# An encoder layer on one core: the first up-projection weights, their sums and one pair's first products moved into the end of the stage before

## The chip, the cores and the metric

The kernel runs on one core of one Trainium2 chip. A core has a matrix engine (TensorE; PE in the profile, its weight loads PEld), VectorE (DVE), ScalarE (ACT), GpSimd (POOL), an engine that only issues transfers (SyncE, SP), and DMA engines that move data between HBM and the core's memory, SBUF. Matrix products are written to PSUM, in banks of 128 x 512 f32.

The metric is the time of one execution in microseconds, as the device measures it. Every kernel was run several times; the median is given with the lowest and the highest.

## What is computed

One layer of an encoder for two sequences of 512 tokens (1024 rows) of width 1024, all in f32. A first part makes `mixed` from a windowed attention branch and a state-space branch; the change lies behind it, in the last two lines:

```python
    x = x + mixed @ w_out                                   # 1024 x 1024
    h2 = rms_norm(x, ln2)
    return x + jnp.square(jax.nn.relu(h2 @ w_up)) @ w_down  # 1024 x 4096, 4096 x 1024
```

## The kernel before

**Products.** Each f32 operand is split into a part that is rounded for the matrix engine (`hi`, a copy on ScalarE) and the remainder (`lo`, a subtraction on VectorE). One product of blocks is then three matmuls, `hi hi`, `hi lo`, `lo hi` (`mm3`, lines 114 to 118, so L116, L117 and L118 of the profile). With four blocks of inner size 128 a product in the up projection is 12 matmuls of 128 x 512.

**The output projection with the norm (L1222 to L1332).** `out_half(x1, sq, t, b)` makes the 128 rows `t` of sequence `sq` for column half `b`: 24 matmuls, then an addition to the residual rows on VectorE (L1238). The halves of `w_out` lie as rounded parts in `w_rows[0]` (pool `wpool`, two tiles tagged `act0` and `act1`, 16 KB per partition each) and `w_rows[1]` (pool `slot_a`, likewise). When both halves of the rows are there they are stored to `x1_scr` (L1325, issued by ScalarE) and normalised by `norm_of`: a square with a row sum on ScalarE (L1255), two small operations on GpSimd that make the power -1/2 (L1257, L1258), and a scaling on VectorE (L1259).

**The turn.** `turn_of` transposes the normalised rows on TensorE (L1273), eight 128 x 128 blocks into two PSUM banks, and `put` writes the rounded part (ScalarE, L1266) and remainder (VectorE, L1267) of the right-hand operands of the up projection. For sequence 0 these are B11 and B21. For sequence 1, which has the other half of the tokens, they are B22 and the combinations T1, T2, T4, T3, made in this order (L1284 to L1293) in two scratch blocks `tt[0]` and `tt[1]`. Each is complete after the turn of the last rows (`t` = 3). The turn of a block of rows is written behind the first `out_half` of the next block, so that TensorE has products to do while the norm is made. For the last rows the cover is `first_products`, below.

**The up projection (L1343 to L1423).** `w_up` comes in 16 pairs of 256 columns, each as a 2 x 2 block `a11 a21 a12 a22` (`raw`, four blocks of 128 x 512, 1 MB in two loads of 512 KB, L1390). A pair needs seven products instead of eight (Strassen's scheme in Winograd's form): p1 = a11 B11, p2 = a21 B21 (the first two of `raw`), p6 = s2 T2, p7 = s3 T3, p5 = s1 T1, p3 = s4 B22, p4 = `raw[:, 3]` T4, with the sums s1 to s4 made by VectorE from the raw blocks (`sums`, L1378 to L1385). `parts` splits a block into a slot of an eight-slot ring (L1346 to L1351, so L1349 on ScalarE and L1350 on VectorE). The results are combined on VectorE (`combine`, L1364), pass a squared ReLU on ScalarE (L1370, L1371) and are stored to `a_scr`.

**Pairs 0 and 1 at the seam.** p1 and p2 of the first two pairs are made in the stage before, by `first_products` (L1296 to L1308): it makes p1, copies it out of PSUM on ScalarE (L1306), makes p2 and adds both on VectorE (L1304). They need only blocks a11 and a21, which are loaded separately (`up_parts`, L1245 to L1250, tile `f_raw`). Pair 0's parts are made early into tiles of their own (`ws`). Pair 1's parts go into `wpool`'s two tiles when `w_rows[0]` is no longer read (`early`, L1327 and L1328). At the end stand: `first_products(ws)`, the last turn, `first_products(ws_1)`. Then `wpool` is closed, and the pool `up` is opened over its memory and that of the stage's work tiles (`rn2`). The whole 1 MB of pair 0 and of pair 1 is then loaded into `up`'s `u_raw` buffers, two of them, and pair 0's sums and parts are made from it.

**What sets the order.** TensorE's order in this stage is the written one (`manual_schedule(engines={ET.PE})`, L1311, until `order.close()`, L1332). On the other engines, and on TensorE in the up projection, a scheduler at compile time takes the written order as priority and puts later work into gaps that it sees. Whatever order results, an engine then keeps it. A tile whose memory was another's waits until that one was last used.

Of the kernel before, what the change touches and what calls it, by code (L numbers as in the profile page):

```python
# [12 lines left out]
F32 = mybir.dt.float32  # L13
# [6 lines left out]
P = 128  # L20
# [4 lines left out]
KT = D // P  # L25
NSEQ = 2
HALF = 512
# [36 lines left out]
def hybrid_layer(ctx, tc, x, rel, onehot, w_qkv, w_ug, vectors, lam, coefs, w_glu, w_out, ln2,  # L64
                 w_up, w_down, out):
    nc = tc.nc
    V, S, PE, GP, SP = nc.vector, nc.scalar, nc.tensor, nc.gpsimd, nc.sync
# [58 lines left out]
    def slot(pool):  # L126
        return [pool.tile([P, KT, HALF], F32R, tag=f"act{i}", name=f"act{i}") for i in range(2)]
# [140 lines left out]
    order = ctx.enter_context(ExitStack())  # L268
# [954 lines left out]
    with tc.tile_pool(name="rn2", bufs=2, reuse_waits="tile") as rn2:  # L1223
        ln2_bc = rn2.tile([P, D], F32, name="ln2_bc", bufs=1)
        SP.dma_start(ln2_bc, ln2.to_broadcast([P, D]))
        for k in range(KT):
            row_piece(w_rows[1], 1, k, rn2.tile([P, HALF], F32, tag="w_raw", name="w_raw", bufs=3))

        def rows_of(sq, t):
            return slice((sq * 4 + t) * P, (sq * 4 + t + 1) * P)  # L1230

        def out_half(x1, sq, t, b):
            ps = acc()
            for k in range(KT):
                mm3(ps, [q[:, k, t * P:(t + 1) * P] for q in mixT[sq]], [q[:, k, :] for q in w_rows[b]],
                    k == 0, k == KT - 1)
            xs = x1[:, b * HALF:(b + 1) * HALF]
            V.tensor_add(xs, ps, xs)  # L1238

        def load_rows_of(sq, t):  # L1240
            x1 = rn2.tile([P, D], F32, tag="x1", name="x1")
            SP.dma_start(x1, x[rows_of(sq, t), :])
            return x1

        def up_parts(r, i, hi, lo):  # L1245
            raw = rn2.tile([P, 4, P], F32, tag="w_raw", name="f_raw", bufs=3)
            SP.dma_start(raw, w_up[r, :, i])
            S.copy(hi, raw)
            V.tensor_sub(lo, raw, hi.bitcast(F32))
            return hi, lo  # L1250

        def norm_of(x1):
            xn = rn2.tile([P, D], F32, tag="xn", name="rn_xn", bufs=1)
            ss = small.tile([P, 1], F32, tag="ss", name="ss")
            S.activation(xn, x1, AF.Square, scale=D ** -0.5, accum_out=ss)  # L1255
            rs = small.tile([P, 1], F32, tag="rs", name="rs")
            GP.tensor_scalar_add(ss, ss, EPS)  # L1257
            GP.tensor_tensor(rs, ss, neg_half[:, 0:1], op=ALU.pow)  # L1258
            V.scalar_tensor_tensor(xn, x1, rs, ln2_bc, op0=ALU.mult, op1=ALU.mult)  # L1259
            return xn  # L1260

        def turn_of(sq, t, xn):
            cs = slice(t * P, (t + 1) * P)

            def put(dst, src):
                S.copy(dst[0][:, :, cs], src)  # L1266
                V.tensor_sub(dst[1][:, :, cs], src, dst[0][:, :, cs].bitcast(F32))  # L1267

            for kq in range(2):
                ps = tps() if sq == 0 else sps()  # L1270
                for i in range(4):
                    kk = kq * 4 + i
                    PE.transpose(ps[:, i * P:(i + 1) * P], xn[:, kk * P:(kk + 1) * P], ident)  # L1273
                xb.append(ps.rearrange("p (k t) -> p k t", k=4))
            if sq == 0:
                put(B11, xb[0])
                put(B21, xb[1])
                return
            tx = rn2.tile([P, 2, 4, P], F32, tag="xn", name="tx", bufs=1)
            tt = [tx[:, 0], tx[:, 1]]  # L1280
            x11, x21, x12, x22 = xb
            put(B22, x22)

            S.copy(tt[0], x11)  # L1284
            V.tensor_sub(tt[0], x12, tt[0])
            put(T1, tt[0])
            V.tensor_sub(tt[1], x22, tt[0])
            put(T2, tt[1])
            V.tensor_sub(tt[1], tt[1], x21)
            put(T4, tt[1])  # L1290
            S.copy(tt[0], x22)
            V.tensor_sub(tt[0], tt[0], x12)
            put(T3, tt[0])  # L1293
            xb.clear()

        def first_products(ws):  # L1296
            sums = []
            for w, b in zip(ws, (B11, B21)):
                ps = acc()
                for k in range(4):  # L1300
                    mm3(ps, [q[:, k, :] for q in w], [q[:, k, :] for q in b], k == 0, k == 3)
                d = fpre.tile([P, HALF], F32, tag="f_lo" if sums else "f_hi", name="f_sum")
                if sums:
                    V.tensor_add(d, ps, sums[0])  # L1304
                else:
                    S.copy(d, ps)  # L1306
                sums.append(d)
            first.append(sums)  # L1308

        xb, owed = [], None  # L1310
        order.enter_context(tc.manual_schedule(engines={ET.PE}))  # L1311
        x1s = [load_rows_of(sq, 0) for sq in range(NSEQ)]
        for sq in range(NSEQ):
            out_half(x1s[sq], sq, 0, 0)
        ws = [up_parts(0, i, *[fpre.tile([P, 4, P], F32R, tag=tag, name=tag) for tag in ("f_hi", "f_lo")]) for i in range(2)]
        for t in range(NT // 2):
            if t:
                x1s = [load_rows_of(sq, t) for sq in range(NSEQ)]
            for sq in range(NSEQ):
                halves = (0, 1) if t else (1,)  # L1320
                for b in halves:
                    out_half(x1s[sq], sq, t, b)
                    if b == halves[0] and owed:
                        turn_of(*owed)
                S.dma_start(x1_scr[rows_of(sq, t), :], x1s[sq])  # L1325
                owed = sq, t, norm_of(x1s[sq])
        early = slot(wpool)  # L1327
        ws_1 = [up_parts(1, i, *[q[:, i, :].rearrange("p (k n) -> p k n", k=4) for q in early]) for i in range(2)]  # L1328
        first_products(ws)
        turn_of(*owed)  # L1330
        first_products(ws_1)
        order.close()  # L1332
    wpool_cm.__exit__(None, None, None)
    front.close()
    ring = slot(slot_a)


    ps_m = ctx.enter_context(tc.tile_pool(name="ps_m", bufs=8, space=PSUM, reuse_waits="tile"))
# [2 lines left out]
        return ps_m.tile([P, HALF], F32, tag="bank", name="bank")  # L1341

    with tc.tile_pool(name="up", bufs=2, reuse_waits="tile") as fp:  # L1343
        turn = itertools.count()

        def parts(src):  # L1346
            i = next(turn) % KT
            hi, lo = [q[:, i, :].rearrange("p (k n) -> p k n", k=4) for q in ring]
            S.copy(hi, src)  # L1349
            V.tensor_sub(lo, src, hi.bitcast(F32))  # L1350
            return hi, lo  # L1351

        def product(a, b):
            w = parts(a)
            ps = bank()
            for k in range(4):
                mm3(ps, [q[:, k, :] for q in w], [q[:, k, :] for q in b], k == 0, k == 3)
            return ps

        ONCE = ("t1", "t2", "t3", "t4", "a12", "a21", "u2", "u3", "u4")  # L1360

        def combine(op, p, q, tag):
            d = fp.tile([P, HALF], F32, tag=tag, name=tag, bufs=1 if tag in ONCE else 2)
            op(d, p, q)  # L1364
            return d

# [8 lines left out]

            S.dma_start(a_scr[n - 1, :, r, :], src)

        def sums(raw):  # L1378
            a11, a12, a21, a22 = [raw[:, i] for i in range(4)]
            sm = [fp.tile([P, 4, P], F32, tag=f"s{i}", name=f"s{i}", bufs=1) for i in range(4)]  # L1380
            V.tensor_add(sm[0], a21, a22)
            V.tensor_sub(sm[1], sm[0], a11)
            V.tensor_sub(sm[2], a11, a21)
            V.tensor_sub(sm[3], a12, sm[1])
            return sm  # L1385

        for r in range(NPAIR):
            raw = fp.tile([P, 4, 4, P], F32, tag="u_raw", name="u_raw")
            for i in range(2):
                SP.dma_start(raw[:, i * 2:i * 2 + 2], w_up[r, :, i * 2:i * 2 + 2])  # L1390
            if r < len(first):
                u1, a11 = first[r]
                S.activation(a11, a11, AF.Relu)
                S.activation(a11, a11, AF.Square)
                s1, s2, s3, s4 = sums(raw)
            else:
                p1 = product(raw[:, 0], B11)
                p2 = product(raw[:, 1], B21)
                s1, s2, s3, s4 = sums(raw)
                u1 = fp.tile([P, HALF], F32, tag="u1", name="u1", bufs=1)  # L1400
                S.copy(u1, p1)
                a11 = relu2(V.tensor_add, p2, u1, "a11")
            put_a(1, a11)
            p6 = product(s2, T2)
            u2 = combine(V.tensor_add, p6, u1, "u2")
            p7 = product(s3, T3)
            u3 = combine(V.tensor_add, p7, u2, "u3")
# [15 lines left out]
            put_a(3, combine(V.tensor_sub, a12, t2, "t4"))  # L1423
    fpre_cm.__exit__(None, None, None)
    t4p_cm.__exit__(None, None, None)
    opers.close()


# [162 lines left out]
```

## Time and profile before

| | |
|---|---|
| time, median of 3 runs | 1502.4 us (1500.92 to 1504.12) |
| the profiled execution | 1503.71 us, its span 1501.9 us |
| mean granted TensorE clock | 0.998 |
| last rows of the output projection, column half 1, matmuls | from 872.7 to 878.5 us of the span |
| p1 and p2 of pair 0, matmuls | 878.3 to 883.9 us |
| the last turn's transposes | 883.75 to 884.8 us |
| p1 and p2 of pair 1, matmuls | 884.5 to 890.25 us |
| first matmul of the pair loop (p6 of pair 0) | 895.16 us |

The profile is that of one execution. All stretches and times within it count from the start of its span. Rows of the timeline give start, length, engine, line, operation, and output and inputs by the names of the tiles; in square brackets stands how long the engine had been idle and what released it. Matmuls overlap in these rows: one is listed with 0.39 us, but the next starts about 0.23 us later. The lengths of DMA rows are those of the issue; the landing is listed apart, in microseconds from the issue.

### The profile page before, as it was taken

To read this page: it belongs to the slowest core of one execution; us is meant where nothing else is said; L and a number is where in the kernel's file an instruction comes from. 1 tells how busy PE (TensorE), PEld (TensorE's weight loads), DVE (VectorE), ACT (ScalarE), POOL (GpSimd) and SP (SyncE) were. 2 spreads that over 40 slices of the span, in tenths; PEclk is the share of its full clock that TensorE was granted. 3 is DMA by queue.
4 is the path that set the end of the run, shared out by engine and by line. 5 is a ranking of instruction groups with operands and counts; after the bars stand their busy time and mean duration, and the time that the engine had idled before them with its cause. 6 is when DMAs were issued, how large, how long until landed. Compare 5 with 4: busy or idle time off the path is not lost.

```text
span 1501.9 us, 22138 instructions
## 1 busy us (share of the span) xinstructions
PE 1453.4 (97%) x8074; PEld 1230.0 (82%) x8074; DVE 1106.8 (74%) x1989; ACT 761.7 (51%) x1362; POOL 212.6 (14%) x372
## 2 busy tenths in 40 slices
PE   6999999999999999999999989999999999999998
PEld 4888888888999888887787868888888888888787
DVE  7998859976646888887975478777777588575653
ACT  6777852235536777775334254445555443433332
POOL 3133341002232443222100000000000000000000
PEclk9999999999999999999999999999999999999999
DMA  4455469229731445275544234444443794454441
GB/s 174 140 169 168 160 208 345 107 100 344 287 132 36 155 135 183 88 252 170 185 135 162 92 115 159 155 154 154 155 154 126 267 352 132 153 182 154 126 123 60
DMA packets 103165, 249.69 MB, mean 166 GB/s; under 512 B 12266, under 2 KB 23786, under 8 KB 103056
## 3 DMA queue, kind: packets, MB, share of 16 engines
q1 hardware_dynamic: 60528, 140.07, 28.7%
q0 software_dynamic: 16896, 53.53, 10.3%
q10 hardware_dynamic: 25632, 54.67, 9.7%
q8 instruction: 64, 1.05, 0.3%
q14 instruction: 45, 0.37, 0.1%
HBM read 173.74 MB, written 90.21 MB: 176 GB/s over the span
## 4 chain that ended last, share of the span: by engine, by line
PE 78%; DVE 8%; ACT 4%; DMA 4%; issue 3%; POOL 1%; ACTq 0%; SPq 0%; DVEq 0%; POOLq 0%
PE acc L185 14%; PE bank L117 13%; PE bank L118 13%; PE bank L116 13%; PE acc L813 4%; PE acc L123 3%; PE acc L117 2%; PE acc L118 2%; PE acc L116 2%; PE sps L547 2%; PE po L896 2%; PE sps L864 1%; PE tps L880 1%; PE sps L645 1%; DMA fac<-rs_scr 1%
## 5 line engine op out<-in xcount | busy, mean ns | idle before, releaser
L185 PE MATMUL acc<-act,c_hi 128*128 128x512 f32 x768 | 249.6, 400 | 1.0 <-DVE act L304 1.0
L117 PE MATMUL bank<-b_lo,a_hi 128*128 128x512 f32 x448 | 174.6, 390 | 1.6 <-DVE b_lo L1460 1.6
L118 PE MATMUL bank<-b_hi,a_lo 128*128 128x512 f32 x448 | 174.3, 389 | 0.0
L116 PE MATMUL bank<-b_hi,a_hi 128*128 128x512 f32 x448 | 173.5, 389 | 0.0
L185 PEld LDWEIGHTS acc<-act,c_hi 128*128 128x128 f32 x768 | 142.2, 189 | 29.1 <-DVE act L304 2.4
L185 PE MATMUL acc<-act,c_lo 128*128 128x512 f32 x384 | 152.5, 397 | 0.0
L1459 ACT CAST a_hi<-d_a 128x1024 fp32r<-128x1024 f32 x56 | 59.0, 1054 | 179.7 <-PE bank L117 176.4
L116 PE MATMUL bank<-act,act 128*128 128x512 f32 x368 | 144.1, 391 | 4.9 <-ACT act L1349 4.9
L117 PE MATMUL bank<-act,act 128*128 128x512 f32 x368 | 143.7, 391 | 0.0
L118 PE MATMUL bank<-act,act 128*128 128x512 f32 x368 | 143.7, 391 | 0.0
L1460 DVE TENSOR_TENSOR a_lo<-d_a,a_hi 128x1024 fp32r<-128x1024 f32 x56 | 68.5, 1224 | 99.9 <-ACT a_hi L1459 99.9
L813 PE MATMUL acc<-w_hi,act 128*128 128x256 f32 x512 | 116.2, 295 | 0.0
L117 PEld LDWEIGHTS bank<-b_lo,a_hi 128*128 128x128 f32 x448 | 84.1, 188 | 20.1 <-DVE b_lo L1460 2.6
L116 PEld LDWEIGHTS bank<-b_hi,a_hi 128*128 128x128 f32 x448 | 84.1, 188 | 17.5
L118 PEld LDWEIGHTS bank<-b_hi,a_lo 128*128 128x128 f32 x448 | 84.1, 188 | 17.3
L813 PEld LDWEIGHTS acc<-w_hi,act 128*128 128x128 f32 x512 | 87.0, 189 | 3.7
L874 ACT ACTIVATE p<-p,nmx 128x257 f32<-128x257 f32 (+1 forms) x128 | 72.1, 563 | 31.2 <-DVE nmx L868 30.2
L116 PEld LDWEIGHTS bank<-act,act 128*128 128x128 f32 x368 | 69.4, 189 | 19.7 <-ACT act L1349 5.3
L123 PE MATMUL acc<-act,gc_hi 128*128 128x512 f32 x256 | 82.6, 401 | 1.8 <-ACT gc_hi L683 1.8
L185 PEld LDWEIGHTS acc<-act,c_lo 128*128 128x128 f32 x384 | 72.4, 189 | 14.0 <-DVE c_lo L176 0.5
L118 PEld LDWEIGHTS bank<-act,act 128*128 128x128 f32 x368 | 69.4, 189 | 14.9 <-DVE act L1350 0.4
L117 PEld LDWEIGHTS bank<-act,act 128*128 128x128 f32 x368 | 69.5, 189 | 14.3
(328 smaller groups left out, 3434.4 us busy)
## 6 DMA issues: line engine op xcount, KB each, us to landing
d_a<-a_scr SPq DMA_DIRECT2D x56, 512.0 KB, 3.6
u_raw<-in_w_up_dram SPq DMA_DIRECT2D x32, 512.0 KB, 5.1
a_scr<-t ACTq DMA_DIRECT2D x64, 256.0 KB, 4.8
k<-in_w_down_dram SPq DMA_DIRECT2D x32, 512.0 KB, 6.4
c_raw<-in_w_ug_dram SPq DMA_DIRECT2D x48, 256.0 KB, 3.7
a_scr<-a ACTq DMA_DIRECT2D x46, 256.0 KB, 2.1
ct_scr<-ctab POOLq DMA_DIRECT2D x16, 576.0 KB, 3.7
ctab_in<-ct_scr POOLq DMA_DIRECT2D x16, 576.0 KB, 7.6
```

The source lines that it names most:

```text
L116: PE.matmul(ps, a[0], b[0], start=first, stop=False)
L117: PE.matmul(ps, a[0], b[1], start=False, stop=False)
L118: PE.matmul(ps, a[1], b[0], start=False, stop=last)
L123: PE.matmul(ps, w[wi][:, k, :], rows[yi], start=k + p == 0, stop=k == KT - 1 and p == 2)
L185: PE.matmul(ps, w[wi][:, k, :], hT[s][hi][:, k, :], start=n == 0, stop=n == 3 * KT - 1)
L547: PE.matmul(ps[:, i * P:(i + 1) * P], bm[:, ri, g, :], u_sb[:, gp * SH + g, :], start=True, stop=True)
L645: PE.matmul(o, ctab[:, g0 % SI + g, ri, 0:T * CH], st[:, ri, g].rearrange("p s k -> p (s k)"), start=False, stop=ri == 1)
L813: PE.matmul(self.ps, hT[sq][act][:, k, col:col + P], w[:, k % 4, :], start=i == 0, stop=i == 3 * KT - 1)
L874: S.activation(p, p, AF.Exp, bias=self.nmx[:, h:h + 1], scale=-1.0, accum_out=self.sums[:, h, self.qb:self.qb + 1])
L896: PE.matmul(self.po, vv, self.hl[i][part], start=i + part == 0, stop=i == self.nkb - 1 and part == 1)
L1459: S.copy(hi, src)
L1460: V.tensor_sub(lo, src, hi.bitcast(F32))
```

## The change

- **Memory.** After column half 0 of the last rows, `wpool`'s two tiles become `raws` (both buffers of the up weights, as halves of one tile) and `held` (the four sums, one `u1`, two `a11`). `wpool` stays open to the end of the up projection. The ring for `parts` is taken from `slot_a` at the same place; its first writes wait for the last product of column half 1.
- **Loads and sums.** The whole 1 MB of pairs 0 and 1 is loaded ahead of the last `out_half`, and pair 0's four sums are written there as well. Pair 1's a11 and a21 aren't loaded a second time.
- **Order.** From there to the end of the stage ScalarE, VectorE and GpSimd keep the written order too.
- **The norm in two.** `norm_of` is divided into `power_of` and the scaling. For the last rows, pair 1's first parts stand between them, the store of the rows behind the scaling, and then pair 1's second parts and the parts of pair 0's s2 (for p6).
- **The turn.** For sequence 1, T3 is made ahead of T4, in every turn. `first_products` is a generator, and in the last turn pair 1's p1 with its copy is written after T2, its p2 with the addition after T3.
- **The pair loop.** Pairs 0 and 1 neither load nor (pair 0) sum, and pair 0's p6 takes the parts that were made ahead. Buffers that lay in `up` now lie in `raws` and `held`; their number is the same.

```diff
-        def norm_of(x1):
+        def power_of(x1):
             xn = rn2.tile([P, D], F32, tag="xn", name="rn_xn", bufs=1)
             ss = small.tile([P, 1], F32, tag="ss", name="ss")
             S.activation(xn, x1, AF.Square, scale=D ** -0.5, accum_out=ss)
             rs = small.tile([P, 1], F32, tag="rs", name="rs")
             GP.tensor_scalar_add(ss, ss, EPS)
             GP.tensor_tensor(rs, ss, neg_half[:, 0:1], op=ALU.pow)
+            return xn, rs
+
+        def norm_of(x1, xn, rs):
             V.scalar_tensor_tensor(xn, x1, rs, ln2_bc, op0=ALU.mult, op1=ALU.mult)
             return xn
 
-        def turn_of(sq, t, xn):
+        def turn_of(sq, t, xn, between=lambda: None):
...
             put(T2, tt[1])
-            V.tensor_sub(tt[1], tt[1], x21)
-            put(T4, tt[1])
+            between()
             S.copy(tt[0], x22)
             V.tensor_sub(tt[0], tt[0], x12)
             put(T3, tt[0])
+            between()
+            V.tensor_sub(tt[1], tt[1], x21)
+            put(T4, tt[1])
             xb.clear()
...
                 sums.append(d)
+                yield
             first.append(sums)
+            yield
+
+        def load_up(r):
+            raw = raws[:, r % 2]
+            for i in range(2):
+                SP.dma_start(raw[:, i * 2:i * 2 + 2], w_up[r, :, i * 2:i * 2 + 2])
+            return raw
+
+        def up_sums(r, which):
+            a11, a12, a21, a22 = [raws[:, r % 2, i] for i in range(4)]
+            sm = [held[:, i] for i in range(4)]
+            for i in which:
+                op, p, q = ((V.tensor_add, a21, a22), (V.tensor_sub, sm[0], a11), (V.tensor_sub, a11, a21),
+                            (V.tensor_sub, a12, sm[1]))[i]
+                op(sm[i], p, q)
+            return sm
...
                 for b in halves:
+                    if t == 3 and sq == 1 and b == 1:
+                        raws, held, ring = wpool.tile([P, 2, 4, 4, P], F32, tag="act0", name="raws"), \
+                            wpool.tile([P, KT, 4, P], F32, tag="act1", name="held"), slot(slot_a)
+                        load_up(0)
+                        order.enter_context(tc.manual_schedule(engines={ET.Activation, ET.DVE, ET.Pool}))
+                        load_up(1)
+                        up_sums(0, range(4))
                     out_half(x1s[sq], sq, t, b)
                     if b == halves[0] and owed:
                         turn_of(*owed)
+                if t == 3 and sq == 1:
+                    break
                 S.dma_start(x1_scr[rows_of(sq, t), :], x1s[sq])
-                owed = sq, t, norm_of(x1s[sq])
-        early = slot(wpool)
-        ws_1 = [up_parts(1, i, *[q[:, i, :].rearrange("p (k n) -> p k n", k=4) for q in early]) for i in range(2)]
-        first_products(ws)
-        turn_of(*owed)
-        first_products(ws_1)
+                owed = sq, t, norm_of(x1s[sq], *power_of(x1s[sq]))
+        scaled = power_of(x1s[1])
+        ws_1 = [parts(raws[:, 1, 0])]
+        xn = norm_of(x1s[1], *scaled)
+        S.dma_start(x1_scr[rows_of(1, 3), :], x1s[1])
+        ws_1.append(parts(raws[:, 1, 1]))
+        early = parts(up_sums(0, ())[1])
+        for _ in first_products(ws):
+            pass
+        second = first_products(ws_1)
+        turn_of(1, 3, xn, lambda: next(second))
+        next(second)
         order.close()
-    wpool_cm.__exit__(None, None, None)
     front.close()
-    ring = slot(slot_a)
...
-        def product(a, b):
-            w = parts(a)
+        def product(a, b, w=None):
+            w = w or parts(a)
...
         for r in range(NPAIR):
-            raw = fp.tile([P, 4, 4, P], F32, tag="u_raw", name="u_raw")
-            for i in range(2):
-                SP.dma_start(raw[:, i * 2:i * 2 + 2], w_up[r, :, i * 2:i * 2 + 2])
+            raw = load_up(r) if r > 1 else raws[:, r]
             if r < len(first):
                 u1, a11 = first[r]
                 S.activation(a11, a11, AF.Relu)
                 S.activation(a11, a11, AF.Square)
-                s1, s2, s3, s4 = sums(raw)
+                s1, s2, s3, s4 = up_sums(r, range(4) if r else ())
...
-            p6 = product(s2, T2)
+            p6 = product(s2, T2, None if r else early)
```

More of the change, by code (lines that the diff above doesn't have):

```diff
@@ L1307, in first_products, with parts @@
                 sums.append(d)
+                yield
             first.append(sums)
+            yield
[12 more added lines that the diff above has]
+            return sm
+        turn = itertools.count()
+        def parts(src):
+            i = next(turn) % KT
+            hi, lo = [q[:, i, :].rearrange("p (k n) -> p k n", k=4) for q in ring]
+            S.copy(hi, src)
+            V.tensor_sub(lo, src, hi.bitcast(F32))
+            return hi, lo
         xb, owed = [], None
@@ L1343, in hybrid_layer @@
     with tc.tile_pool(name="up", bufs=2, reuse_waits="tile") as fp:
[L1344 to L1351, printed above, removed]
-        def product(a, b):
-            w = parts(a)
+        def product(a, b, w=None):
+            w = w or parts(a)
             ps = bank()
@@ L1358, in product @@
             return ps
-        ONCE = ("t1", "t2", "t3", "t4", "a12", "a21", "u2", "u3", "u4")
         def combine(op, p, q, tag):
-            d = fp.tile([P, HALF], F32, tag=tag, name=tag, bufs=1 if tag in ONCE else 2)
+            if tag == "a11":
+                d = held[:, 5 + r % 2].rearrange("p k n -> p (k n)")
+            else:
+                d = fp.tile([P, HALF], F32, tag=tag, name=tag, bufs=2 if tag == "a22" else 1)
             op(d, p, q)
@@ L1376, in put_a @@
             S.dma_start(a_scr[n - 1, :, r, :], src)
[L1378 to L1385, printed above, removed]
         for r in range(NPAIR):
-            raw = fp.tile([P, 4, 4, P], F32, tag="u_raw", name="u_raw")
-            for i in range(2):
-                SP.dma_start(raw[:, i * 2:i * 2 + 2], w_up[r, :, i * 2:i * 2 + 2])
+            raw = load_up(r) if r > 1 else raws[:, r]
             if r < len(first):
@@ L1398, in hybrid_layer @@
                 p2 = product(raw[:, 1], B21)
-                s1, s2, s3, s4 = sums(raw)
-                u1 = fp.tile([P, HALF], F32, tag="u1", name="u1", bufs=1)
+                s1, s2, s3, s4 = up_sums(r, range(4))
+                u1 = held[:, 4].rearrange("p k n -> p (k n)")
                 S.copy(u1, p1)
@@ L1425, in hybrid_layer @@
     t4p_cm.__exit__(None, None, None)
+    wpool_cm.__exit__(None, None, None)
     opers.close()
```

## The prediction

> **What bounds the kernel now.** I read the page first, then who waited for whom on TensorE, then the busy time in stretches, then the timeline around the one wait that the change touches.
>
> ```profile
> span 1501.9 us, 22138 instructions
> PE 1453.4 (97%) x8074; PEld 1230.0 (82%) x8074; DVE 1106.8 (74%) x1989; ACT 761.7 (51%) x1362; POOL 212.6 (14%) x372
> PE 78%; DVE 8%; ACT 4%; DMA 4%; issue 3%; POOL 1%; ACTq 0%; SPq 0%; DVEq 0%; POOLq 0%
> ```
>
> TensorE is busy 97% of the span and makes 78% of the chain that ended last. No product is removed by the change, so it can only win where TensorE stands still. Of the waits of TensorE (waited-for instruction, total, times, longest), one lies in the part that is changed:
>
> ```profile
> PE bank L116 <- ACT act L1349: 4.9, 1, 4.9
> ```
>
> It is one wait, ahead of the up projection's first product. The stretches around it (columns: length, busy time of each engine, granted clock, DMA share, GB/s):
>
> ```profile
> 890.25:895.16 4.91, 0.00 (x1) 0.01 (x1) 4.91 (x9) 4.42 (x8) 0.00 (x0) 1.00 0.49 190
> 895.16:898.68 3.52, 3.52 (x8) 2.59 (x9) 3.52 (x7) 0.84 (x2) 0.00 (x0) 0.52 0.00 0
> 898.68:960.00 61.32, 61.32 (x272) 50.75 (x271) 51.07 (x81) 31.25 (x52) 0.00 (x0) 1.00 0.44 155
> ```
>
> For 4.91 us TensorE does nothing while VectorE and ScalarE are full. Then eight matmuls take 3.52 us, at a granted clock of 0.52. Later 272 matmuls take 61.32 us, 0.225 each. At that pace the eight would have taken 1.80, so the hole costs 4.91 + 3.52 - 1.80 = 6.6 us, and TensorE stands as if it had begun the stage, at full clock, at 898.68 - 1.80 = **896.88**. That is the reference for all that follows.
>
> What fills the hole:
>
> ```profile
> 889.86 0.39 PE L118 MATMUL acc<-act,act 128*128 128x512 f32 x1
> 895.16 0.79 PE L116 MATMUL bank<-act,act 128*128 128x512 f32 x1 [4.91 <-ACT act L1349]
> ...
> 892.32 0.69 DVE L1381 TENSOR_TENSOR s<-u_raw 128x512 f32<-128x512 f32 x1
> 892.92 0.68 DVE L1383 TENSOR_TENSOR s<-u_raw 128x512 f32<-128x512 f32 x1
> 893.53 0.69 DVE L1382 TENSOR_TENSOR s<-s,u_raw 128x512 f32<-128x512 f32 x1
> 893.45 1.65 ACT L1349 CAST act<-s 128x512 fp32r<-128x512 f32 x3
> ```
>
> The first product (p6) needs the rounded parts of s2. That sum (L1382) starts at 893.53, behind all of the last turn, and its rounding on ScalarE follows. The weights themselves were late:
>
> ```profile
> SPq L1390 <- DVE rn_xn L1259: 23.4, 1, 23.4
> 883.06 1.29 SPq L1390 DMA_DIRECT2D u_raw<-in_w_up_dram  x3
> u_raw<-in_w_up_dram SPq DMA_DIRECT2D x1, 512.0 KB, 5.6
> u_raw<-in_w_up_dram SPq DMA_DIRECT2D x2, 512.0 KB, 6.0
> ```
>
> Their load waits for the normalised rows, whose memory the buffers share. The first 512 KB land 5.6 us after issue; 6.0 is the middle of the first two, so the second took 6.4.
>
> **The change, part by part.** *Loads.* The two tiles that hold output-weight column half 0 come free with the last product of that half:
>
> ```profile
> 871.93 0.62 ACT L1248 CAST act<-f_raw 128x512 fp32r<-128x512 f32 x1 [2.44 <-PE acc L118]
> ```
>
> Here a rounding into the same tiles was released at 871.93. The new loads, two halves for pair 0 and two for pair 1, are issued from about 872.0, 11 us earlier. Pair 1's two blocks, until now among four separate loads, no longer have loads of their own:
>
> ```profile
> L1247 SPq DMA_DIRECT2D f_raw<-in_w_up_dram x4: 328/328/328, 795.9 to 801.0; - x4
> ```
>
> Those went out 70 us ahead of the hole, on a queue that nothing here waits for, so their end is worth nothing.
>
> *Sums.* The four sums of pair 0 stand in VectorE's written order ahead of the addition that ends the last output rows (L1238). They need both halves of pair 0's load. What a second half takes, beside the 6.4 above:
>
> ```profile
> 922.91 0.80 SPq L1390 DMA_DIRECT2D u_raw<-in_w_up_dram  x2
> u_raw<-in_w_up_dram SPq DMA_DIRECT2D x1, 512.0 KB, 5.5
> ```
>
> Issues are 0.43 and 0.40 apart, so the second half lands 5.9 to 6.8 us after the first issue: at 877.9 to 878.8. I take the middle, 878.3. Four sums at the 0.60 spacing of L1381 to L1382 hold VectorE for 2.4, to **880.7**.
>
> The Trainium skill, "DMA: Bandwidth & Descriptors", section "Anatomy of one DMA", gives another price: a fixed 2.0 us plus the bytes over 436 GB/s, which makes 3.2 for one 512 KB load and, as an estimate, 4.4 for two behind each other. By it the sums would start near 876.4 and delay nothing. The trace's 5.5 to 6.4 disagree, and the sum goes by them.
>
> *The last rows.* Their chain now:
>
> ```profile
> 878.51 0.69 DVE L1238 TENSOR_TENSOR x<-acc,x 128x512 f32<-128x512 f32 x1 [3.43 <-PE acc L118]
> 879.23 0.33 ACTq L1325 DMA_DIRECT2D x_scr<-x  x1
> 879.61 1.06 ACT L1255 ACTIVATE rn_xn<-x 128x1024 f32<-128x1024 f32 x1 [5.56 <-DVE x L1238]
> 881.15 0.57 POOL L1258 TENSOR_TENSOR rs<-ss,neg_half 128x1 f32<-128x1 f32 x1
> 881.75 1.29 DVE L1259 SCALAR_TENSOR_TENSOR rn_xn<-x,rs,ln_bc 128x1024 f32<-128x1024 f32 x1 [2.55 <-POOL rs L1258]
> 883.75 1.03 PE L1273 MATMUL sps<-ident,rn_xn 128*128 128x128 f32 x8
> 884.54 0.48 PE L116 MATMUL acc<-act,act 128*128 128x512 f32 x1
> ```
>
> From the addition's start to the normalised rows' end took 4.53 (878.51 to 883.04), and TensorE came to the transposes at 883.75, so there was 0.7 of slack. The change writes the store of the rows (0.38 of ScalarE ahead of the square) after the square, and puts one rounding remainder between the power and the scaling on VectorE. That remainder waits for its cast, which follows the square on ScalarE, and costs 0.26 more than the power's own wait. So 4.4 us instead of 4.53. With the addition at 880.7 instead of 878.51 the rows are ready at 885.1, and the transposes start at **885.1**, 1.35 late. TensorE has nothing else in its written order for that time.
>
> *The second pair's products.* They follow the transposes as before, with parts that are cast by then: from the first transpose to the first product 0.79 (883.75 to 884.54), and 24 matmuls from 884.54, the last starting at 889.86, so 0.231 each and 5.55 in all. TensorE is free for p6 at 885.1 + 6.34 = **891.44**.
>
> *p6's operands.* The parts of s2 are now made ahead of the turn. The moving operand T2 becomes the last one needed, since the written order holds VectorE to put T1's remainder ahead of the subtraction for T2. Pieces of that chain in the turn of before:
>
> ```profile
> 886.50 0.68 DVE L1285 TENSOR_TENSOR tx<-sps,tx 128x512 f32<-128x512 f32 x1
> 887.27 1.29 ACT L1266 CAST act<-tx 128x512 fp32r<-128x512 f32 x2 [0.40 <-DVE tx L1285]
> 887.92 1.36 DVE L1267 TENSOR_TENSOR act<-tx,act 128x512 fp32r<-128x512 f32 x2
> ```
>
> A cast follows its subtraction by 0.09, and a remainder follows its cast closely. After the transposes (885.1 + 1.03): two copies out of PSUM 1.1, subtraction behind B22's remainder 0.9, cast 0.7, remainder 0.7, subtraction 0.6, cast 0.7, remainder 0.7: 5.4 to 5.5, thus 891.6. p6's first matmul needs only T2's cast, its second the remainder, at 891.67. No stall, but no slack either.
>
> *What is late next.* Two small terms. ScalarE and VectorE take work of the up loop into the turn's gaps, which I bound by 0 and 1.0 (nearest row: two parts of 0.62 and 0.69 less what the gaps hold) and put at 0.3. And the second sum of pair 1's first products now stands behind T3; p7 needs that sum's PSUM bank and T3's remainder, and I put it at 0.5 (one 0.69 instruction; bounds 0 and 1.4). T3 ahead of T4 fits the order in which p7 and p4 read them. In earlier turns neither is read, so that swap costs nothing there.
>
> *Clock.* Remaining idle pieces are about 1.4 and some tenths. The nearest such piece in the trace kept its clock:
>
> ```profile
> 805.98 0.33 PE L1273 MATMUL tps<-ident,rn_xn 128*128 128x128 f32 x1 [1.05 <-DVE rn_xn L1259]
> 804.00:807.00 3.00, 1.95 (x14) 1.45 (x13) 1.89 (x2) 0.33 (x1) 0.58 (x1) 1.00 0.28 113
> ```
>
> So the 1.7 us of slow matmuls go with the hole. Should the pieces join to something nearer 4.91, they stay.
>
> *Sum.* p6 effectively at 891.44 + 0.3 + 0.5 = 892.2 against 896.88: **4.6 us** less. The profiled execution took 1503.7, 1.8 outside its span of 1501.9 and 1.3 above the median of 1502.4. It becomes 1499.1 and the median **1497.8**.
>
> *After that.* Loads and sums of pairs 2 to 15 keep their number, size and double buffering; only the addresses change. They cost nothing as long as a load may start when its own half is read.
>
> **The rivals.** *Loads quicker than I take them.* If the second half lands by 876.9, the addition is not delayed, the transposes start at 883.75 and p6 effectively at 890.9: 6.0 us, 1496.4. For it: the loads meet no other traffic at 872. Against: the rows of 5.5 and 6.4. This is also what the skill's price gives.
>
> *Up work stays behind the turn.* If nothing of the up loop enters the gaps, p7 waits for the parts of s3 until T4's remainder (16 us after the addition's start by the chain above) and a cast and remainder more: about 3.6 us of stall, a gain of 1.0, 1501.4. Against it, an earlier end of a written order:
>
> ```profile
> L981 DVE TENSOR_TENSOR w_lo<-w_in,w_hi x8: 681/684/687, 421.4 to 427.6; 128x512 fp32r<-128x512 f32 x8
> L238 DVE TENSOR_TENSOR keys<-acc,rk x8: 424/425/426, 387.7 to 425.4; 128x256 f32<-128x256 f32 x8
> ```
>
> L238 is in a written order, L981 is free and written later, and yet its first starts at 421.4, before the last L238 at 425.4.
>
> *A shared wait in the weights' one tile (slower).* Both buffers are now halves of one tile. If a load had to wait for the reads of both halves, pair 3's load would go out when pair 2's last part is read instead of a pair earlier:
>
> ```profile
> 941.95 0.33 SPq L1390 DMA_DIRECT2D u_raw<-in_w_up_dram  x1
> u_raw<-in_w_up_dram SPq DMA_DIRECT2D x1, 512.0 KB, 4.6
> 943.90 0.68 DVE L1364 TENSOR_TENSOR a<-u,bank 128x512 f32<-128x512 f32 x1
> L1349 ACT CAST act<-u_raw x44: 607/623/626, 892.9 to 1168.9; 128x512 fp32r<-128x512 f32 x44
> ```
>
> Its first half would land at 946.6 and be cast at 947.2, while TensorE is done with pair 2 at about 943.8: 3.4 us, in some 13 pairs 44, less the 4.6: 1542. It decides as soon as a load goes out less than about 5 us before its pair. Against it: the ring of parts is one tile too, its slices are written (the 44 casts) while others are read, and TensorE shows no wait there from 898.68 to 960.
>
> **How the numbers follow.** Forecast 0.52; quicker loads 0.14; up work behind the turn, or loads some 2 us later than I take them, 0.24; shared wait, or another new stall of several us, 0.10. About 0.2%, 3 us, is what a measurement of this kernel can tell from no change. So faster 0.66, same 0.24, slower 0.10. The range reaches from the whole hole gone (6.6: 1495.8) to a gain of nearly nothing, 1495.6 to 1502.2, and leaves out the slower cases.
>
> **What would show it.** Right: four loads issued near 872; L1238's last addition near 880.7, transposes near 885, p6 near 891.5 at a clock of 1.00, and a hole ahead of the transposes in place of the one ahead of p6. Wrong: transposes at 883.75 (quick loads), p7 waiting for a part of s3 (up work behind), TensorE waiting for a load in later pairs (shared wait), or a clock near 0.5 again.

## The result, and the profile after

| | before | changed |
|---|---|---|
| time, median | 1503.37 us (18 runs, 1500.92 to 1507.67) | 1497.53 us (18 runs, 1494.94 to 1500.23) |
| ratio to before | | 0.9962 (95% interval 0.9954 to 0.9970) |
| span of the profiled execution | 1501.9 us | 1494.5 us |

The change takes 5.8 us, by the interval 4.5 to 6.9. The forecast was 4.6.

The page of the changed kernel, its span, its busy times and the chain that ended last:

```profile
span 1494.5 us, 22155 instructions
PE 1450.9 (97%) x8074; PEld 1227.6 (82%) x8074; DVE 1106.4 (74%) x1989; ACT 760.8 (51%) x1362; POOL 212.9 (14%) x372
PE 78%; DVE 9%; DMA 5%; ACT 4%; issue 3%; POOL 1%; SPq 0%; ACTq 0%; DVEq 0%; POOLq 0%
```

Counts of instructions on the engines are the same and busy times nearly so. What went is idle time, and the slow matmuls that stood behind it. The list of TensorE's waits between 870 and 960 us shows the first (total, times, longest); before, one wait of 4.9 stood there:

```profile
PE sps L1276 <- DVE rn_xn L1262: 0.6, 1, 0.6
PE bank L116 <- ACT f_sum L1311: 0.5, 1, 0.5
PE bank L117 <- DVE act L1270: 0.2, 1, 0.2
```

The rows of the timeline behind these (in the changed kernel the turn's transposes are L1276, `put` is L1269 and L1270, the sums L1329, `parts` L1337 and L1338, `first_products` L1309 and L1311):

```profile
870.33 1.78 SPq L1320 DMA_DIRECT2D raws<-in_w_up_dram  x4
870.34 0.69 DVE L1238 TENSOR_TENSOR x<-acc,x 128x512 f32<-128x512 f32 x1 [0.16 <-PE acc L118]
...
875.56 0.69 DVE L1329 TENSOR_TENSOR held<-raws 128x512 f32<-128x512 f32 x1 [2.67 <-DMA raws<-in_w_up_dram]
...
878.10 0.68 DVE L1238 TENSOR_TENSOR x<-acc,x 128x512 f32<-128x512 f32 x1
878.70 1.88 DVE L1338 TENSOR_TENSOR act<-held,act 128x512 fp32r<-128x512 f32 x3
...
879.15 1.06 ACT L1255 ACTIVATE rn_xn<-x 128x1024 f32<-128x1024 f32 x1 [0.31 <-DVE x L1238]
...
880.84 0.69 DVE L1338 TENSOR_TENSOR act<-raws,act 128x512 fp32r<-128x512 f32 x1 [0.25 <-ACT act L1337]
...
881.45 1.28 DVE L1262 SCALAR_TENSOR_TENSOR rn_xn<-x,rs,ln_bc 128x1024 f32<-128x1024 f32 x1
...
882.88 1.06 PE L1276 MATMUL sps<-ident,rn_xn 128*128 128x128 f32 x8 [0.58 <-DVE rn_xn L1262]
...
889.92 0.50 PE L116 MATMUL bank<-act,act 128*128 128x512 f32 x1 [0.50 <-ACT f_sum L1311]
890.59 0.50 PE L117 MATMUL bank<-act,act 128*128 128x512 f32 x1 [0.16 <-DVE act L1270]
890.93 0.40 PE L118 MATMUL bank<-act,act 128*128 128x512 f32 x1
```

All times of this part are best counted from the last product of column half 0, which frees the memory: the addition at 870.34 here, at 871.93 before. The loads go out at once, the sums start 5.2 us later, the last addition after 7.8 (before: 6.6), the transposes after 12.5 (before: 11.8), and p6 after **19.6** (before: 23.2). Behind p6 the clock stays up (length, busy times, granted clock):

```profile
889.92:900.00 10.08, 9.91 (x42) 7.97 (x43) 10.05 (x18) 5.54 (x10) 0.00 (x0) 1.00 0.26 89
```

A measure of the whole seam is the time from that last half-0 product to the last matmul of the up projection, the end of p4 of pair 15 (first and last start of this group; before, then changed):

```profile
L118 PE MATMUL bank<-t,act x64: 389/389/389, 908.2 to 1190.4; 128*128 128x512 f32 x64
```

```profile
L118 PE MATMUL bank<-t,act x64: 389/389/390, 901.9 to 1184.1; 128*128 128x512 f32 x64
```

1190.4 - 871.93 = 318.5 before, 1184.1 - 870.34 = 313.8 now: **4.7 us** less. I call it the stretch below. The spans differ by 7.4, but 1.6 of that lies ahead of the seam and 1.1 behind it, in code that is the same; the last experiment shows how far such parts move by themselves.

### The profile page after: what moved, and what is told of

Its sections match the earlier page's. It is cut to its first block, busy times and chain, and to the rows that moved or that the text cites. A ratio compares the mean times of both kernels' runs of the same rounds, so it can differ in the third digit from the quotient of the medians.

```text
span 1494.5 us, 22155 instructions
## 1 busy us (share of the span) xinstructions
PE 1450.9 (97%) x8074; PEld 1227.6 (82%) x8074; DVE 1106.4 (74%) x1989; ACT 760.8 (51%) x1362; POOL 212.9 (14%) x372
## 4 chain that ended last, share of the span: by engine, by line
PE 78%; DVE 9%; DMA 5%; ACT 4%; issue 3%; POOL 1%; SPq 0%; ACTq 0%; DVEq 0%; POOLq 0%
PE acc L185 14%; PE bank L117 13%; PE bank L118 13%; PE bank L116 13%; PE acc L813 4%; PE acc L123 3%; PE sps L547 2%; PE acc L117 2%; PE acc L118 2%; PE acc L116 2%; PE po L896 2%; PE sps L864 1%; PE sps L645 1%; PE tps L880 1%; DMA fac<-rs_scr 1%
```

## The experiments

Theory A: the late load of pair 0's weights was the cause. Once they lie there before the last turn, VectorE and ScalarE get to the sums and parts in time, whoever orders them. Theory B: what wins is that the sums and parts are written ahead and the order of the engines is fixed. In the table, p6 is counted from the last half-0 product of the same execution; "before" is the kernel before on the same chip.

| run | time, us | before, us | ratio (95%) | p6 after, us | longest hole, us | stretch, us |
|---|---|---|---|---|---|---|
| before | | | | 23.2 | 4.9 | 318.5 |
| changed | 1497.53 | 1503.37 | 0.9962 (0.9954 to 0.9970) | 19.6 | 0.6 | 313.8 |
| loads_alone | 1496.03 | 1502.68 | 0.9951 (0.9936 to 0.9967) | 18.3 | 0.3 | 312.5 |
| loads_only | 1497.28 | 1502.68 | 0.9957 (0.9944 to 0.9970) | 20.3 | 1.5 | 314.4 |
| free_order | 1496.74 | 1502.68 | 0.9957 (0.9940 to 0.9974) | 18.3 | 0.3 | 312.9 |
| no_between | 1504.12 | 1502.68 | 1.0010 (0.9996 to 1.0024) | 24.5 | 5.3 | 320.0 |
| late_load | 1505.39 | 1503.26 | 1.0011 (0.9999 to 1.0024) | 20.3 | 3.2 | 319.3 |
| copy_late | 1500.69 | 1503.26 | 0.9984 (0.9967 to 1.0002) | 21.8 | 2.9 | 315.5 |
| two_sums_copy_early | 1496.83 | 1503.26 | 0.9960 (0.9944 to 0.9976) | 19.3 | 1.0 | 313.6 |
| t4_first | 1503.95 | 1503.26 | 1.0003 (0.9990 to 1.0016) | 19.6 | 2.6 | 320.5 |
| loads_alone_again | 1497.85 | 1505.81 | 0.9952 (0.9934 to 0.9970) | 18.2 | 0.3 | 312.4 |
| changed_again | 1498.87 | 1505.81 | 0.9965 (0.9953 to 0.9976) | 19.5 | 0.5 | 313.6 |

### The early loads alone

The changed kernel with the new memory, the early loads and the norm in two (with the store of the rows behind the scaling); the rest is taken back:

```diff
                         load_up(0)
-                        order.enter_context(tc.manual_schedule(engines={ET.Activation, ET.DVE, ET.Pool}))
                         load_up(1)
-                        up_sums(0, range(4))
...
-        early = parts(up_sums(0, ())[1])
...
-        turn_of(1, 3, xn, lambda: next(second))
-        next(second)
+        turn_of(1, 3, xn)
+        for _ in second:
+            pass
...
-                s1, s2, s3, s4 = up_sums(r, range(4) if r else ())
+                s1, s2, s3, s4 = up_sums(r, range(4))
...
-            p6 = product(s2, T2, None if r else early)
+            p6 = product(s2, T2)
```

and T4 ahead of T3 again in `turn_of`. Pair 1's first parts still come from the one early load.

> Of the change only the memory and the early loads are kept: sums and s2's parts stand in the pair loop again, ScalarE, VectorE and GpSimd have no written order, T4 stands ahead of T3, pair 1's first products are written behind the whole turn. Theory A (the late load was the cause; once the weights lie there at 875, VectorE and ScalarE get to the sums and parts by themselves, ahead of the last turn): p6 starts 18.5 to 20 us after the last half-0 product, against 19.6 in the changed kernel and 23.2 before, clock 1.00, about 1497.5 us. Theory B (the written order and the sums made ahead are what wins; without them VectorE, which is full from 882 to 900, makes them behind the turn as before): p6 at 22 us or later with a clock near 0.5, 1501 to 1503 us.

Theory A holds: p6 after 18.3 us, a little earlier than it said, and ratio 0.9951. VectorE and TensorE in the timeline of this run, where the last half-0 product ends at 870.44:

```profile
875.74 1.29 DVE L1327 TENSOR_TENSOR held<-raws 128x512 f32<-128x512 f32 x2 [2.75 <-DMA raws<-in_w_up_dram]
876.95 0.69 DVE L1327 TENSOR_TENSOR held<-held,raws 128x512 f32<-128x512 f32 x1
877.55 0.68 DVE L1238 TENSOR_TENSOR x<-acc,x 128x512 f32<-128x512 f32 x1
...
882.36 1.06 PE L1276 MATMUL sps<-ident,rn_xn 128*128 128x128 f32 x8
...
888.75 0.39 PE L116 MATMUL bank<-act,act 128*128 128x512 f32 x1
889.47 0.50 PE L117 MATMUL bank<-act,act 128*128 128x512 f32 x1 [0.33 <-DVE act L1270]
```

Nobody wrote the sums there. The scheduler put three of the four into the gap ahead of the last addition and the fourth behind it. The transposes start without a hole, and of the old hole 0.33 us is left. This smaller edit has the shortest stretch of all.

### The written order with the loads, and the free order with all the rest

`loads_only` is the changed kernel without the line `up_sums(0, range(4))` and without the parts made ahead (`early`); order and products inside the turn stay.

> The changed kernel without the sums and s2's parts made ahead by hand; early loads, written order of the engines and the products inside the turn are kept. Theory A: as the changed kernel, p6 at 19 to 20.5 us after the last half-0 product, 1497 to 1498.5 us. Theory B: 1500 us or more.

p6 after 20.3 us, 1497.28 us: theory A again, with a little loss. The hole of 1.5 us ahead of p6 is a wait for the copy of pair 1's p1 (L1311), which the written order holds behind T2's cast. On ScalarE, ahead of that cast, stood a part of the pair loop that waited for a ring slot:

```profile
889.11 0.62 ACT L1337 CAST act<-held 128x512 fp32r<-128x512 f32 x1 [1.57 <-PE acc L117]
889.63 0.62 ACT L1269 CAST act<-tx 128x512 fp32r<-128x512 f32 x1
890.15 0.58 ACT L1311 COPY f_sum<-acc 128x512 f32<-128x512 f32 x1
```

`free_order` is the changed kernel without the line that fixes the order of ScalarE, VectorE and GpSimd.

> The changed kernel without the written order on ScalarE, VectorE and GpSimd. Theory A: no loss; the copy of pair 1's p1 is no longer held behind T2's cast and T2's subtraction no longer behind T1's remainder, so p6's wait of 0.5 us goes: p6 at 18.8 to 19.6 us, 1496.5 to 1497.5 us. Theory B: up-loop work gets ahead of the turn, p6 later by 1 to 3 us, 1498.5 to 1501 us.

p6 after 18.3 us, half a microsecond earlier than theory A had it, and the stretch 0.9 us shorter than with the order. So the written order gains nothing here; in the seam it costs about a microsecond.

### The load held back

loads_alone with one thing undone. `load_up(0)` is moved behind the scaling, and GpSimd first writes one element of each half of the buffer from the scaled rows, which the load overwrites:

```diff
-                        load_up(0)
                         load_up(1)
...
+        for i in (0, 2):
+            GP.tensor_copy(raws[:, 0, i, 0, 0:1], xn[:, 0:1])
+        load_up(0)
         S.dma_start(x1_scr[rows_of(1, 3), :], x1s[1])
```

> loads_alone with one thing undone: pair 0's load is held back until the last rows are normalised (GpSimd writes one element of each half of the buffer from them first), as it was before the change; pair 1's stays early. If the late load is the whole cause, its second half lands some 6 us after the normalised rows, at 17.5 us after the last half-0 product, sums and s2's parts follow: p6 at 22 to 25 us, a hole of 4 to 6 us, clock near 0.5, 1502 to 1505 us. If the memory or the other order of the engines carries the gain: p6 at 20 us or earlier and 1498 us or less.

The gain is gone: 1505.39 us, ratio 1.0011. The number for p6 is a miss, since the first two matmuls slipped in and the hole came in two pieces (TensorE, then stretches with the granted clock):

```profile
891.17 0.50 PE L116 MATMUL bank<-act,act 128*128 128x512 f32 x1 [1.94 <-ACT act L1335]
891.51 0.40 PE L117 MATMUL bank<-act,act 128*128 128x512 f32 x1
895.05 0.80 PE L116 MATMUL bank<-act,act 128*128 128x512 f32 x1 [3.15 <-ACT act L1335]
```

```profile
891.90:895.05 3.15, 0.01 (x2) 0.00 (x1) 3.15 (x7) 2.62 (x6) 0.00 (x0) 0.56 0.10 36
895.05:898.50 3.45, 3.45 (x8) 2.77 (x9) 3.45 (x6) 0.55 (x1) 0.00 (x0) 0.50 0.60 195
```

Both pieces wait for a cast of the pair loop, as the hole before the change did; VectorE had waited for the load until 887.65 to make the first sum. The time lies just above the 1502 to 1505 us that were expected for a late load. The two kernels differ in pair 0's load alone: in the free order its early start is necessary. It is also enough there, together with the new memory and the norm in two, which both kernels keep and which gain nothing without it.

### Pair 1's products behind the turn

```diff
-        turn_of(1, 3, xn, lambda: next(second))
-        next(second)
+        turn_of(1, 3, xn)
+        for _ in second:
+            pass
```

> The changed kernel with pair 1's first products written behind the whole turn, the written order kept. If p6's PSUM bank is that of pair 1's p1 (the wait of 0.5 us for the copy L1311 says so), p6 has to wait for a copy that now stands behind T4's cast on ScalarE: p6 at 24 to 25.5 us after the last half-0 product, a hole of 4.5 to 6 us, granted clock near 0.5 behind it, 1503 to 1505 us, so the whole gain lost. If the banks don't tie them: p6 at 20 us, 1498 us.

```profile
893.54 0.79 PE L116 MATMUL bank<-act,act 128*128 128x512 f32 x1 [5.31 <-ACT f_sum L1311]
```

```profile
893.54:897.10 3.56, 3.56 (x8) 2.81 (x9) 2.51 (x5) 1.26 (x2) 0.00 (x0) 0.50 0.04 15
```

The hole of 5.3 us and the clock of 0.50 came as the tie of the banks says: TensorE waits for nothing but the copy L1311. Under the written order the products inside the turn are worth the whole gain. In the free order they are worth nothing, as loads_alone shows, which has them behind the turn too: there the scheduler places the copy (886.98) ahead of T2's cast (887.65), while under the written order of no_between it comes at 892.91, behind T4's cast.

### A smaller hole, and the clock

In `turn_of` the first `between()` is moved from behind `put(T2)` to behind `put(T3)`, so that the copy of pair 1's p1 comes later.

> The changed kernel with the copy of pair 1's p1 out of PSUM written behind T3's cast instead of behind T2's. ScalarE reaches it about 2 to 2.5 us later, so p6 begins 21.5 to 22.3 us after the last half-0 product, behind a hole of 2.5 to 3.1 us. If a hole of that size leaves the clock at 1.00, the loss is that hole's 2 to 2.5 us alone: about 1499.8 us, matmuls of p6 at 0.23 us each. If the clock falls as it did behind 4.9 us, 1.7 us more: 1501.5 us, matmuls at 0.43 us.

```profile
892.84 0.50 PE L116 MATMUL bank<-act,act 128*128 128x512 f32 x1 [2.92 <-ACT f_sum L1311]
893.17 0.39 PE L117 MATMUL bank<-act,act 128*128 128x512 f32 x1
```

```profile
892.84:896.30 3.46, 3.46 (x15) 2.88 (x16) 3.46 (x7) 2.18 (x4) 0.00 (x0) 1.00 0.14 56
```

The median, 1500.69 us, lies between the two forecasts, 1499.8 and 1501.5, and can't decide between them; the trace can. A hole of 2.9 us leaves the clock at 1.00, and the matmuls behind it come 0.23 us apart. The stretch is 1.7 us longer than in the changed kernel. The hole at p6 is 2.4 longer; 0.2 came back at the transposes (a hole of 0.4 instead of 0.6), and some 0.4 inside p6, whose second and third matmul find T2's remainder there.

### The two small holes that are left

Only the two sums that s2 needs stay ahead of the last addition, and the copy moves ahead of T2's cast:

```diff
-                        up_sums(0, range(4))
+                        up_sums(0, range(2))
...
-        early = parts(up_sums(0, ())[1])
+        early = parts(up_sums(0, (2, 3))[1])
...
+            between()
             put(T2, tt[1])
-            between()
```

> The changed kernel, written order kept, with only the two sums that s2 needs ahead of the last addition (the other two behind the normalised rows) and the copy of pair 1's p1 ahead of T2's cast. If the delay of the transposes (0.7 us) comes from the sums in front of the addition and p6's wait of 0.5 us from the copy's place, both go: transposes 11.8 to 12.1 us after the last half-0 product with no hole, p6 at 18.3 to 18.9 us with at most 0.4 us for T2's remainder, 1.0 to 1.3 us less than the changed kernel: 1496.3 us. If GpSimd's power or the loads of pair 1 set the transposes, they stay at 12.5 us and the time at 1497.5 us.

Half a miss. The delay of the transposes did come from the sums: they start 11.8 us after the last half-0 product (884.27 - 872.43), with no hole. But p6 starts only 0.2 us earlier than in the changed kernel, and waits for T2's cast:

```profile
884.27 1.03 PE L1276 MATMUL sps<-ident,rn_xn 128*128 128x128 f32 x8
...
891.76 0.50 PE L116 MATMUL bank<-act,act 128*128 128x512 f32 x1 [1.00 <-ACT act L1269]
```

```profile
890.57 0.62 ACT L1337 CAST act<-held 128x512 fp32r<-128x512 f32 x1 [1.36 <-PE acc L117]
891.09 0.61 ACT L1269 CAST act<-tx 128x512 fp32r<-128x512 f32 x1
```

The second fence is ScalarE: a cast of the pair loop, put ahead of T2's cast, waits 1.36 us for its ring slot, which pair 1's products still read. An engine keeps its order, so T2 waits with it.

### T4 ahead of T3

The changed kernel with T4 ahead of T3 in `turn_of`, the second `between()` between them.

> The changed kernel with T4 ahead of T3 again in every turn of sequence 1 (pair 1's p1 behind T2, its p2 behind T4). T3 is then cast some 2 us later in the last turn. If p7 is bound by T3, TensorE waits 1 to 2 us there: 1498.5 to 1499.5 us. If T3 has slack, no wait and 1497.5 us.

p7 is bound by T3, but where 1 to 2 us of loss was expected the whole gain is gone: ratio 1.0003, the stretch 6.7 us longer than in the changed kernel. The wait is larger, and the clock falls:

```profile
896.69 0.51 PE L116 MATMUL bank<-act,act 128*128 128x512 f32 x1 [2.61 <-ACT act L1269]
897.85 0.80 PE L117 MATMUL bank<-act,act 128*128 128x512 f32 x1 [0.66 <-DVE act L1270]
```

```profile
898.00:900.00 2.00, 2.00 (x5) 1.61 (x6) 1.69 (x3) 0.00 (x0) 0.00 (x0) 0.50 0.00 0
```

T3's subtraction was done at 895.4, but its cast came at 896.03, behind two steps of the pair loop on ScalarE (L1418 at 894.83, L1419 at 895.49). Under the written order, then, this swap of two lines is as much a condition of the gain as the early load is. In loads_alone T4 stands ahead of T3 and TensorE has no such wait.

### Both versions once more

The kernels of loads_alone and of the changed kernel on one chip.

> The kernel of loads_alone once more, beside the changed kernel on one chip. In its first trace the stretch from the last half-0 product to the last matmul of the up projection was 312.5 us against 313.8 in the changed kernel and 318.5 before. If the smaller edit is as good or better, that stretch is again 312.3 to 312.9 us, and the time 1 to 1.5 us below the changed kernel's, which the medians may not resolve; if the first trace flattered it, 313.5 us or more and no lower time.

> The changed kernel itself, unedited, for that comparison: the stretch 313.5 to 314.1 us, holes of about 0.6 and 0.7 us at the transposes and at p6, the time 5 to 6 us below the kernel before.

The stretches repeat within 0.2 us: 312.4 and 313.6. The medians are 1.0 us apart, in the same direction, with intervals that overlap. So the smaller edit is ahead of the changed kernel by 1.3 us in the seam; in the whole time this isn't resolved. The changed kernel's gain here, 6.9 us, is above the 5 to 6 that were expected.

The profiled execution of changed_again has a span of 1501.6 us, 7.1 above that of the changed kernel, from the same code. The seam isn't the place: 6.8 us of it lie ahead of the last half-0 product (877.10 against 870.34). Two stretches there, in changed_again and in the changed kernel:

```profile
690.00:700.00 10.00, 8.12 (x34) 6.35 (x34) 5.73 (x14) 4.63 (x13) 1.09 (x1) 0.83 0.36 134
800.00:840.00 40.00, 39.95 (x172) 31.67 (x172) 21.02 (x29) 13.19 (x24) 3.20 (x8) 0.92 0.33 116
```

```profile
690.00:700.00 10.00, 9.29 (x46) 7.46 (x47) 5.95 (x15) 6.37 (x14) 2.34 (x3) 1.00 0.36 117
800.00:840.00 40.00, 39.34 (x189) 32.41 (x188) 21.86 (x30) 14.21 (x25) 3.20 (x8) 1.00 0.29 105
```

Its granted clock fell there in this one execution. Two single spans can't be subtracted to judge a change of 5 us; the stretch, counted from a point inside the execution, can.

## Why the prediction was right, point by point

The forecast was 1497.8 us and a gain of 4.6; the median is 1497.53, and the seam gained 4.7. That the time itself came within 0.3 us is partly luck: the median before is 1503.37 in 18 runs, 1.0 above the three runs that the forecast started from, and the measured gain is larger by 1.2. The remaining 1 us of the measured 5.8 is not located, and lies within the interval.

- **The hole and its price: right.** The one wait of 4.9 us and the slow matmuls behind it are gone, and the clock stays at 1.00. That the clock is part of the price is shown by no_between (hole 5.3, clock 0.50) against copy_late (hole 2.9, clock 1.00): against the changed kernel, the first lost 6.2 us of stretch by a hole 4.8 us longer, the second 1.7 by one 2.4 longer.
- **The loads: too long by 1.1 us.** I took 6.3 us from the first issue to the sums, it was 5.2. So the rival of quicker loads was half true. The price of the Trainium skill, "DMA: Bandwidth & Descriptors", section "Anatomy of one DMA", gave 4.4 as an estimate; the Trainium skill states it for transfers issued by GpSimd, and these are issued by SyncE. The measurement lies between the two. The loads met no other traffic than pair 1's loads behind them, which I had named and not weighed.
- **The addition and the transposes: right in kind.** The addition came 1.2 us later than before where I had 2.2, and TensorE stood still 0.6 us ahead of the transposes where I had 1.35. two_sums_copy_early shows that the sums do this. From the addition to the normalised rows it took 4.6 (878.10 to 882.73) instead of 4.4. I had credited 0.38 for the store that no longer stands ahead of the square, but the square began 0.37 after the addition's end (879.15), nearly as before (0.41); why is open. The remainder between the power and the scaling (880.84) cost about 0.1 where I had 0.26. Three remainders of the pair loop went into the wait for the power (878.70) and delayed nothing: VectorE stood idle for 0.25 after them.
- **p6's time: right, by two errors that cancel.** I forecast 19.5 us after the release for its operands, and 0.3 more for work in the gaps; it was 19.6. The transposes were 0.6 us earlier than forecast, and p6 then waited 0.5 for the copy of pair 1's p1 and 0.16 for T2's remainder. I gave the bank term to p7 and pair 1's p2. It belonged to p6 and pair 1's p1; p7 doesn't wait.
- **The swap of T3 and T4: undervalued.** I wrote that it fits the order of p7 and p4, and gave it no price. Under the written order it is worth 6.7 us of stretch, as t4_first shows.
- **What carries the gain: not separated.** The sum credited the early load and the sums and parts written ahead together. Only the load was needed, with the memory for it and, for all the runs show, the norm in two. The rows of L981 and L238, which I used against the rival "up work stays behind the turn", say just that: the scheduler moves such work into gaps by itself.
- **The rivals.** Up work did enter the gaps (878.70). A shared wait of the two buffers did not occur: between 870 and 960 us TensorE has the three small waits shown and no other, from there to the end of the up projection it has none, and the stretch is not longer.

## What to carry to other kernels

When an engine stands still at a seam between two stages, look first at what held back the earliest transfer, here memory that was shared with the last work of the stage before; giving that load a home that comes free sooner was enough for the whole gain (with the norm in two, which no run took back by itself), as the free order then moved the sums and parts forward. An order written by hand around it must be complete: each copy out of PSUM that a later product needs, and each operand in the order in which it is read, or a line or two in the wrong place give the whole gain back. Measure such a change between two points inside an execution, as spans of single executions differed by 7 us for the same code.

## What was not expected of the hardware

**Here the clock went with idle time over a stretch, not with one hole.** Single holes of 1.5 us (loads_only) and 2.9 us (copy_late) left it at 1.00; holes of 4.9 (before) and 5.3 us (no_between) brought it to about 0.5. But 2.6 us, one matmul and 0.7 us more also did (t4_first), and so did 1.9 us, two matmuls and 3.2 us (late_load), where the clock fell at 892.3, only 0.4 us into the second hole. The Trainium skill, "TensorE: Matmul & The Clock Gate", section "What's actually happening", has the clock fall after an idle window of about 3.4 us, with windows that run freely. The holes of 1.5, 2.9 and 4.9 us agree with that; the other three cases do not, if the window has to be empty. In no_between the clock fell at 890.7, 2.5 us after the matmuls had stopped, in late_load and t4_first 3.0 and 3.1 us after the first hole began. By an estimate from the Trainium skill's 3.4 us and these rows, the last window ahead of the fall held 0.8 to 1.1 us of matmuls in each of the three.

**What the fall costs depends on when it comes.** Eight matmuls were slow behind the holes before, in no_between and in late_load, but 14 in t4_first, from 897.85 to 904.0 us. The granted clock stood at 0.50 from about 895.0 to 898.5 before (3.5 us), from 890.7 to 897.6 in no_between, from 892.3 to 899.1 in late_load and from 897.2 to 904.0 in t4_first (6.8 to 6.9 us each). In no_between and late_load TensorE stood still for the first 2.8 us of that, in t4_first for 0.6. So the low time of t4_first was no longer than theirs; more of it met matmuls. Why it was only half as long before is open.
